# A fused two-block transformer kernel: the places of SBUF tiles modulo 1024 bytes, set by the tiles' role in a matmul

## The chip, the core and the metric

One core of one Trainium2 chip runs the whole kernel. The metric is the device time of one execution in microseconds. [...] SBUF has 128 partitions, and a tile's place is its start address in bytes within a partition; every tile here starts at the same address in all partitions.

## The reference

Two blocks run one after the other on a sequence of 256 tokens with 1024 features, all in float32. Cut to what matters here:

```python
# first block
hn = rms_norm(h, g);  proj = hn @ w_in                  # w_in: 1024 x 8192
merged = sum of three gated branches (spatial gating, convolution, pooling)
h = h + rms_norm(merged @ w_out, g)
f = (silu(hn @ w_gate) * (hn @ w_up)) @ w_ffn_out       # 1024 x 5632, 2816 x 1024
h = h + rms_norm(f, g);  h = h + sigmoid(h @ w_ple_gate) * (p @ w_ple)
# second block, two layers
x = layer_norm(alpha * x + mixer(x))                    # retention, then latent attention
q = x @ w_q;  s = q . sub_keys;  top 16 of 256 candidates per head (8 heads)
h = gelu(u[eidx] . x);  y = sum(gate * h * v[eidx])     # 16384 experts, u and v: 16384 x 1024
x = layer_norm(alpha * x + y)
```

The expert layer (twice) is computed densely: all 16384 rows of `u` meet all tokens, the gates are zero for the experts that a token did not choose, and all 16384 rows of `v` are summed.

## The kernel before

**Weights.** All weights come through one stream (`units`, a list in the order of use). Each unit is a 128x1024 float32 tile: SyncE loads it into one of four `raw` buffers (L139), ScalarE copies it, rounded, into one of three `whi` buffers (L149), and VectorE writes the rest, `raw - whi`, into one of three `wlo` buffers (L164). The activations are split in the same way into a high and a low part. A float32 product is then three TensorE matmuls in the type fp32r: high x high, high x low, low x high.

**Two kinds of matmul.** In every matmul one operand is stationary (128 columns, loaded into the array by a weight load, a PEld record) and one is moving (streamed past it, a MATMUL record). Each matmul has its own weight load, also where the operand is the same as before, and the load for the next matmul runs while this one streams.

- `mm3` (L221 to L223), used by `lin_fm` and by the `u` half of the expert layers: the stationary operand is 128 columns of `whi` or `wlo`, the moving one is 256 tokens of an activation tile (`hl`, `hl3b`, `hlp`, `cqhl`, `phl`). Below: 256-wide. 10,608 matmuls.
- `tm_half` (L285 to L287), used by `lin_tm` and by the `v` half of the expert layers: the stationary operand is 128 tokens of an activation tile (`hl`, `fhl`, `yhl`, `cqhl`, `ohl`, and in the expert layers `ch` and `cl`), the moving one is 512 columns of `whi` or `wlo`. Below: 512-wide. 3072 of them read `ch` and `cl`, 264 `fhl`, 192 `yhl`, 528 `hl`, 96 `ohl`, 42 `cqhl`.

In an expert layer the stretch that reads `u` (256-wide, 128 tiles of weights, 24 matmuls each) comes first, the stretch that reads `v` (512-wide, 128 tiles, 12 matmuls each) second. In the first of them score matmuls (`X` and `q`, float32) and short runs of eight float16 matmuls (`o` with `ohh` and `ohl`, 128 wide) stand between the runs of 24.

**What sets the places.** Tiles are taken from pools. A pool gives out addresses in the order in which its tiles are first asked for, each rounded up to 32 bytes, and the pools `const`, `keep`, `wst` (the weight buffers), `sm` and then those of the stages lie one behind the other. So the place of a tile follows from the sizes of all the tiles ahead of it. `const` starts at byte 16,512. The tile `hl` of the pool `keep` is at byte 21,472 (992 modulo 1024), the weight buffers start at byte 38,944, and since each has 4096 bytes, all ten are at 32 modulo 1024. A slice of 128 columns starts 512 bytes after the one before, a row of 256 tokens 1024 bytes.

The order of the work is written out by hand (weights two units ahead, background work in generators), and nothing in it depends on an address.

Of the kernel before, what the change touches and what calls it, by code (L numbers as in the profile page):

```python
# [10 lines left out]
F32 = mybir.dt.float32  # L11
F32R = mybir.dt.float32r
F16 = mybir.dt.float16
I32 = mybir.dt.int32
# [5 lines left out]
P = 128  # L20
# [72 lines left out]
def fused_kernel(ctx: ExitStack, tc: tile.TileContext, a: dict, out: bass.AP):  # L93
# [3 lines left out]
    const = ctx.enter_context(tc.tile_pool(name="const", bufs=1))  # L97
    keep = ctx.enter_context(tc.tile_pool(name="keep", bufs=1))
    wst = ctx.enter_context(tc.tile_pool(name="wst", bufs=1))
    sm = ctx.enter_context(tc.tile_pool(name="sm", bufs=2))  # L100
# [11 lines left out]

    idle = const.tile([P, 384], F16, name="idle")
    nc.vector.memset(idle, 1.0)

    def C(name, n=None):
        o = COFF[name]
        return cst[:, o:o + (n or dict(CSTS)[name])]
# [217 lines left out]
            nc.vector.scalar_tensor_tensor(out=y, in0=t, scalar=1.5, in1=y, op0=ALU.add, op1=ALU.mult)  # L336
        return y

    eps_t = const.tile([P, 2], F32, name="eps_t")
    nc.vector.memset(eps_t[:, 0:1], EPS1)  # L340
    nc.vector.memset(eps_t[:, 1:2], EPS2)

    def table_ready(func=AF.Sqrt):

        nc.scalar.activation(out=small("rt", 1), in_=eps_t[:, 0:1], func=func)
# [34 lines left out]
    def coeffs_of(mv, eps, root=False, ahead=False):  # L380

        x, nm = small("rx", 2), small("nm", 2)
        if root:
            r = rstd_root(mv[:, :, 1], 1.0, eps, ahead)
        else:
            nc.vector.tensor_scalar(out=x, in0=mv[:, :, 1], scalar1=eps, scalar2=None, op0=ALU.add)
            r = rstd_of(x, 2)
        nc.vector.scalar_tensor_tensor(out=nm, in0=mv[:, :, 0], scalar=-1.0, in1=r, op0=ALU.mult, op1=ALU.mult)
        return r, nm
# [18 lines left out]
    def ax():  # L408
        return ps_ax.tile([P, 512], F32, tag="ax", name="ax")
# [58 lines left out]
    def sincos(ang, sn, cs, pool, n, c1=0.9, c2=1.2):  # L468

        k = pool.tile([P, n], F32, tag="sck", name="sck")  # L470
        nc.vector.tensor_scalar(out=k, in0=ang, scalar1=1.0 / TWO_PI, scalar2=None, op0=ALU.mult)
        nc.vector.tensor_scalar(out=k, in0=k, scalar1=MAGIC, scalar2=None, op0=ALU.add)
        nc.vector.tensor_scalar(out=k, in0=k, scalar1=-MAGIC, scalar2=None, op0=ALU.add)
        yield c1
        for c in (C1, C2, C3):
            nc.vector.scalar_tensor_tensor(out=ang, in0=k, scalar=-c, in1=ang, op0=ALU.mult, op1=ALU.add)
        yield c2
        nc.vector.tensor_scalar(out=ang, in0=ang, scalar1=float(np.float32(3.1415925)), scalar2=float(np.float32(-3.1415925)), op0=ALU.min, op1=ALU.max)
        yield None
        nc.scalar.activation(out=k, in_=ang, func=AF.Abs)  # L480
        nc.scalar.activation(out=sn, in_=ang, func=AF.Sin)
        yield None
        nc.vector.tensor_scalar(out=k, in0=k, scalar1=-1.0, scalar2=math.pi / 2, op0=ALU.mult, op1=ALU.add)
        yield None
        nc.scalar.activation(out=cs, in_=k, func=AF.Sin)
        yield None
# [104 lines left out]
    acct = mx.tile([P, 2, 2, 512], F32, tag="cacct", name="acct")  # L591

    def conv_stats():
        bs = sm.tile([P, 2, 2, 6], F32, tag="cbs", name="cbs", bufs=1)
        for g in range(2):
            while ready["a"] < 4 * g + 4:
                yield None
            yield None
            yield None
            for b in range(2):  # L600
                ps = ax()
                for k in range(4):
                    nc.tensor.transpose(ps[:, k * P:(k + 1) * P], acc[:, 4 * g + k, b * P:(b + 1) * P], ident)
                yield None
                nc.vector.bn_stats(out=bs[:, b, g, :], in_=ps)
                nc.scalar.activation(out=acct[:, g, b, :], in_=ps, func=AF.Copy)
                yield 0.6
        mv = sm.tile([P, 2, 2], F32, tag="mv", name="mv")
        for b in range(2):
            nc.vector.bn_aggr(out=mv[:, b, :], in_=bs[:, b])  # L610
        r, nm = coeffs_of(mv, EPS1, root=True)
        yield 1.6
        for g in range(2):
            nc.scalar.activation(out=acct[:, g, 0, :], in_=acct[:, g, 0, :], func=AF.Identity, scale=r[:, 0:1], bias=nm[:, 0:1])
            nc.vector.tensor_scalar(out=acct[:, g, 1, :], in0=acct[:, g, 1, :], scalar1=r[:, 1:2], scalar2=nm[:, 1:2], op0=ALU.mult, op1=ALU.add)
            yield 0.6
        table_ready(AF.Silu)

    bg += [conv_stats(), conv_taps()]
    lin_fm("w_conv", hl, KD, 16, ev_conv, head=2, produce=[pr_x, pr_x2], budget=BUD["w_conv"], x32=hn32)  # L620

# [108 lines left out]
    for gi in range(4):  # L730
        for f in range(2):
            c = 2 * gi + f
            gp = bank(c % 4)[:, :T]
            for k in range(2):
# [3 lines left out]
                s = slice((t % 8) * P, (t % 8 + 1) * P)  # L738
# [104 lines left out]
    ff, fhl = ff_box["p"], ff_box["fhl"]  # L843
# [38 lines left out]
    decay = tb.tile([P, 4, 2 * T], F32, tag="decay", name="decay")  # L882
    bg.append(tables())
    pT = ff.tile([P, 2, T], F32, name="pT")
    phl = ff.tile([P, 2, 2, T], F32R, name="phl")
    nc.gpsimd.dma_start(out=pT, in_=a["pT"])

# [18 lines left out]
    def ev_ple(i):  # L906
        nc.scalar.activation(out=pple[:, 2 * i:2 * i + 2, :].rearrange("p a t -> p (a t)"), in_=pps[i], func=AF.Copy)

    for f in range(8):
        for k in range(2):  # L910
# [6 lines left out]
            s = slice((t % 8) * P, (t % 8 + 1) * P)  # L917
            mm3(pps[f // 2][:, (f % 2) * T:(f % 2 + 1) * T], (w[0][:, s], w[1][:, s]), (phl[:, 0, k, :], phl[:, 1, k, :]), k == 0, k == 1)
    ev_ple(2)
    ev_ple(3)  # L920
    hlp = ff.tile([P, 2, KD, T], F32R, name="hlp")

    def pr_h2(k):
# [467 lines left out]
        return hl2_box["lt"].after  # L1391


    sc2 = keep.tile([P, 2, 2, 1, 32], F32, name="sc2")
    sn2, cs2 = sc2[:, 0], sc2[:, 1]

    def angles():
        posc = keep.tile([P, 2], I32, name="posc")
        nc.gpsimd.dma_start(out=posc, in_=a["posc"])
        posf = keep.tile([P, 2], F32, name="posf")  # L1400
        ang = keep.tile([P, 64], F32, name="angm")
        for _ in range(16):
            yield None
        nc.vector.tensor_copy(out=posf, in_=posc)
        for b in range(2):
            nc.vector.tensor_scalar(out=ang[:, b * 32:(b + 1) * 32], in0=C("invf64"), scalar1=posf[:, b:b + 1], scalar2=None, op0=ALU.mult)
        yield 2.5
        yield from sincos(ang, sn2.rearrange("p b o f -> p (b o f)"), cs2.rearrange("p b o f -> p (b o f)"), keep, 64, 2.5, 2.5)

    PE0, X = peer(0, hl, lt, hm, [RT, TB], after0, beside_v=[angles()])  # L1410
    lt, hl, hm = hl2_box["lt"], hl2_box["hl"], hl2_box["hm"]

# [14 lines left out]
    ml = ML.enter_context(tc.tile_pool(name="ml", bufs=1))  # L1427
# [5 lines left out]
    for b in range(2):  # L1433
        nc.scalar.activation(out=kvr[:, b, 0:128], in_=psb[b][0][:, 384:512], func=AF.Copy)
        nc.scalar.activation(out=kvr[:, b, 128:320], in_=psb[b][1][:, 0:192], func=AF.Copy)
    cqhl = ml.tile([P, 2, 5, T], F32R, name="cqhl")

    def cq_t(k):
# [8 lines left out]
        cq_t(k)  # L1447

    mjunk = ml.tile([P, 512], F32, name="mjunk")
    rqs = ml.tile([P, 2], F32, name="rqs")  # L1450
    SCL = 192.0 ** -0.5
    ss, x4 = small("ss4", 4), small("x4", 4)

# [281 lines left out]
```

## Time and profile before

| | |
|---|---|
| three timed runs | 2524.02 us median (2523.16 to 2529.32) |
| the profiled execution | 2526.07 us, its span 2524.3 us |
| TensorE, matmuls | 2482.1 us busy (98%), 16,903 records |
| TensorE, weight loads | 2236.3 us (89%), 16,903 records |
| VectorE | 1815.6 us (72%) |
| ScalarE | 1276.8 us (51%) |
| DMA | 441.14 MB, mean 175 GB/s |
[...]

How to read it: a matmul's record reaches from its start to the end of its output, and the next one starts long before that end, so the durations of matmuls overlap and their sum is more than the span. What a matmul costs the engine is the step from its start to the start of the next one. It is taken below from the first and the last start of many like matmuls. Where the steps of two runs of the same shape differ, the durations differ by about as much.

### The profile page before, as it was taken

The page shows a single profiled execution, that of the slowest core. Times are in us where ns is not written, and L with a number is a line of the kernel's source. Part 1 is how long each engine was busy: PE and PEld are TensorE (multiplying, and loading weights), DVE is VectorE, ACT ScalarE, POOL GpSimd, SP SyncE. Part 2 cuts the span into 40 slices and gives each one's busy share as a digit, 9 for nine tenths or more (in the row PEclk, how much of TensorE's full clock was granted, in tenths as well). Part 3 has the DMA queues.
Part 4 walks back from the last instruction along what each step waited for, and adds up shares of the span by engine and source line. Part 5 has one row for each costly group of instructions (what it writes and reads, how often), then busy time and mean ns, then how long its engine had stood idle before and what let it go on. Part 6 is the DMA issues. An engine that isn't in the chain of part 4 may idle for free.

```text
span 2524.3 us, 43428 instructions
## 1 busy us (share of the span) xinstructions
PE 2482.1 (98%) x16903; PEld 2236.3 (89%) x16903; DVE 1815.6 (72%) x3714; ACT 1276.8 (51%) x2161; POOL 9.2 (0%) x21
## 2 busy tenths in 40 slices
PE   8999999999999999999999999999999999999998
PEld 8899899898889999999878888779999999888886
DVE  7988677676656978899555555666978998555555
ACT  5544555563544555544454444544565554444444
POOL 0000000000000000000000000000000000000000
PEclk9999999999999999999999999999999999999999
DMA  6645556555454554545655555525654445655553
GB/s 205 219 147 169 176 164 195 188 192 175 133 177 167 178 190 162 163 163 164 203 184 186 190 187 167 166 77 180 193 191 159 161 160 169 221 187 190 186 190 117
DMA packets 120927, 441.14 MB, mean 175 GB/s; under 512 B 13936, under 2 KB 14320, under 8 KB 119312
## 3 DMA queue, kind: packets, MB, share of 16 engines
q1 hardware_dynamic: 118832, 425.91, 51.8%
q0 software_dynamic: 1888, 12.45, 1.4%
q8 instruction: 132, 2.16, 0.3%
q14 instruction: 75, 0.61, 0.1%
HBM read 433.07 MB, written 5.24 MB: 174 GB/s over the span
## 4 chain that ended last, share of the span: by engine, by line
PE 82%; issue 13%; DMA 2%; ACT 2%; DVE 1%; SPq 0%; POOL 0%; POOLq 0%; ACTq 0%; DVEq 0%
PE bank L287 11%; PE bank L285 11%; PE bank L286 11%; PE bank L221 10%; PE bank L222 10%; PE bank L223 10%; PE lps L221 4%; PE lps L222 4%; PE lps L223 4%; PE lps L270 2%; PE ax L1273 1%; PE ax L1274 1%; DMA X<-in_keys_dram 1%; PE ax L1112 1%; ACT whi L149 1%
## 5 line engine op out<-in xcount | busy, mean ns | idle before, releaser
L164 DVE TENSOR_TENSOR wlo<-raw,whi 128x1024 fp32r<-128x1024 f32 (+1 forms) x797 | 968.1, 1216 | 529.3 <-ACT whi L149 526.7
L149 ACT ACTIVATE whi<-raw 128x1024 fp32r<-128x1024 f32 (+1 forms) x797 | 838.7, 1053 | 723.0 <-PE bank L287 477.4
L221 PE MATMUL bank<-hl,whi 128*128 128x256 f32 x2080 | 597.7, 287 | 4.0 <-ACT hl L550 3.0
L222 PE MATMUL bank<-hl,whi 128*128 128x256 f32 x2080 | 584.7, 281 | 0.3
L223 PE MATMUL bank<-hl,wlo 128*128 128x256 f32 x2080 | 584.4, 281 | 0.3 <-DVE wlo L164 0.3
L285 PE MATMUL bank<-whi,ch 128*128 128x512 f32 x1024 | 404.9, 395 | 1.9 <-ACT ch L323 1.9
L287 PE MATMUL bank<-whi,cl 128*128 128x512 f32 x1024 | 404.8, 395 | 0.1
L286 PE MATMUL bank<-wlo,ch 128*128 128x512 f32 x1024 | 404.5, 395 | 0.0
L221 PEld LDWEIGHTS bank<-hl,whi 128*128 128x128 f32 x2080 | 394.4, 190 | 4.8 <-ACT hl L550 3.3
L222 PEld LDWEIGHTS bank<-hl,whi 128*128 128x128 f32 x2080 | 395.4, 190 | 1.4 <-DVE hl L465 0.5
L223 PEld LDWEIGHTS bank<-hl,wlo 128*128 128x128 f32 x2080 | 392.7, 189 | 1.0 <-DVE wlo L164 0.9
L221 PE MATMUL lps<-hl,whi 128*128 128x256 f32 x1208 | 343.0, 284 | 0.6 <-ACT fhl L834 0.5
L223 PE MATMUL lps<-hl,wlo 128*128 128x256 f32 x1208 | 337.1, 279 | 0.5 <-DVE wlo L164 0.5
L222 PE MATMUL lps<-hl,whi 128*128 128x256 f32 x1208 | 336.9, 279 | 0.0
L285 PEld LDWEIGHTS bank<-whi,ch 128*128 128x128 f32 x1024 | 191.9, 187 | 49.1 <-ACT ch L323 2.8
L287 PEld LDWEIGHTS bank<-whi,cl 128*128 128x128 f32 x1024 | 191.9, 187 | 48.7 <-DVE cl L324 1.8
L286 PEld LDWEIGHTS bank<-wlo,ch 128*128 128x128 f32 x1024 | 191.9, 187 | 46.7
L221 PEld LDWEIGHTS lps<-hl,whi 128*128 128x128 f32 x1208 | 228.9, 189 | 1.5 <-ACT fhl L834 0.7
L222 PEld LDWEIGHTS lps<-hl,whi 128*128 128x128 f32 x1208 | 229.5, 190 | 0.3
L223 PEld LDWEIGHTS lps<-hl,wlo 128*128 128x128 f32 x1208 | 228.7, 189 | 0.8 <-DVE wlo L164 0.7
L1302 ACT ACTIVATE gel<-bank 128x84 f32<-128x84 f32 (+47 forms) x154 | 44.0, 286 | 178.6 <-PE bank L223 178.6
L1304 ACT ACTIVATE X<-bank 128x256 f32<-128x256 f32 (+33 forms) x246 | 76.5, 311 | 105.8 <-PE bank L223 105.8
(420 smaller groups left out, 3063.9 us busy)
## 6 DMA issues: line engine op xcount, KB each, us to landing
raw<-in_p_u_dram SPq DMA_DIRECT2D x256, 512.0 KB, 3.3
raw<-in_p_v_dram SPq DMA_DIRECT2D x256, 512.0 KB, 3.4
raw<-in_w_fi_dram SPq DMA_DIRECT2D x44, 512.0 KB, 4.2
raw<-in_p_q_dram SPq DMA_DIRECT2D x32, 512.0 KB, 3.4
raw<-in_w_gate_dram SPq DMA_DIRECT2D x24, 512.0 KB, 3.3
raw<-in_w_fo_dram SPq DMA_DIRECT2D x22, 512.0 KB, 3.7
raw<-in_w_conv_dram SPq DMA_DIRECT2D x16, 512.0 KB, 4.2
raw<-in_r_qk_dram SPq DMA_DIRECT2D x16, 512.0 KB, 4.2
```

Source lines behind the costliest of these rows:

```text
L149: nc.scalar.activation(out=hi[:, :c], in_=raws[j][:, :c], func=AF.Copy)
L164: nc.vector.tensor_tensor(out=lo[:, :c], in0=r[:, :c], in1=hi[:, :c].bitcast(F32), op=ALU.subtract)
L221: nc.tensor.matmul(ps, w[0], x[0], start=start, stop=False, skip_group_check=True)
L222: nc.tensor.matmul(ps, w[0], x[1], start=False, stop=False, skip_group_check=True)
L223: nc.tensor.matmul(ps, w[1], x[0], start=False, stop=stop, skip_group_check=True)
L270: nc.tensor.matmul(ps[:, :T], w[0][:, s], x32[:, k0 + k, :], start=(k == 0), stop=(k == nk - 1), skip_group_check=True)
L285: nc.tensor.matmul(ps[:, :n], xh, w[0][:, o:o + n], start=first, stop=False, skip_group_check=True)
L286: nc.tensor.matmul(ps[:, :n], xh, w[1][:, o:o + n], start=False, stop=False, skip_group_check=True)
L287: nc.tensor.matmul(ps[:, :n], xl, w[0][:, o:o + n], start=False, stop=last, skip_group_check=True)
L1112: nc.tensor.matmul(p2[:, b * P:(b + 1) * P], q[:, b * P:(b + 1) * P], box["keys"][:, f, :], start=True, stop=True, skip_group_check=True)
L1302: nc.scalar.activation(out=gl_[:, 0:td], in_=ps[:, 0:td], func=AF.Gelu)
L1304: nc.scalar.activation(out=X[:, e, td:], in_=ps[:, td:T], func=AF.Gelu)
```

## The change

No instruction is added, removed or moved: on every engine the two programs as built hold the same instructions with the same shapes and the same waits in the same order. One VectorE copy, of the 128x2 positions, writes into two spare columns of `eps_t` and no longer into a tile `posf`. Only addresses differ. Three unused tiles (`gap1`, `gap2`, `gap3`) and some larger tiles (`cbs`, `sc2`, `rqs`, `eps_t`) shift what comes behind them, and `posc` moves into `const`.

| tile | role | before, modulo 1024 | after |
|---|---|---|---|
| `raw`, `whi`, `wlo` | both | 32 | 64 |
| `hl` of `keep`, `hl3b` | moving, stationary | 992 | 0 |
| `hl` of the first block's branches | moving, stationary | 960 | 0 |
| `hlp` | moving | 128 | 0 |
| `cqhl` | moving, stationary | 512 | 0 |
| `phl` | moving | 0 | 0 |
| `ch`, `cl` | stationary | 0 | 64 |
| `fhl`, `yhl` | stationary | 0 | 64 |
| `ohl` | stationary | 544 | 64 |
| `X`, `q`, `o`, `ohh` and the expert layers' other tiles | float32, float16 | 0 | 64 |

Since slices of weights and of stationary activations start 512 bytes apart, their places repeat modulo 512: `ohl` at 544 has slices at 32 and at 544, as the weights have.

```diff
@@ -112,6 +112,8 @@
     idle = const.tile([P, 384], F16, name="idle")
     nc.vector.memset(idle, 1.0)
+    eps_t = const.tile([P, 4], F32, name="eps_t")
+    posc = const.tile([P, 2], I32, name="posc")
...
-    eps_t = const.tile([P, 2], F32, name="eps_t")
     nc.vector.memset(eps_t[:, 0:1], EPS1)
     nc.vector.memset(eps_t[:, 1:2], EPS2)
...
     def conv_stats():
-        bs = sm.tile([P, 2, 2, 6], F32, tag="cbs", name="cbs", bufs=1)
+        bs = sm.tile([P, 32], F32, tag="cbs", name="cbs", bufs=1)[:, 0:24].rearrange("p (b g s) -> p b g s", b=2, g=2)
...
     pT = ff.tile([P, 2, T], F32, name="pT")
+    ff.tile([P, 240], F32, name="gap1")
     phl = ff.tile([P, 2, 2, T], F32R, name="phl")
...
     ev_ple(3)
+    ff.tile([P, 224], F32, name="gap2")
     hlp = ff.tile([P, 2, KD, T], F32R, name="hlp")
...
-    sc2 = keep.tile([P, 2, 2, 1, 32], F32, name="sc2")
+    sc2 = keep.tile([P, 144], F32, name="sc2")[:, 0:128].rearrange("p (a b o f) -> p a b o f", a=2, b=2, o=1)
...
     def angles():
-        posc = keep.tile([P, 2], I32, name="posc")
         nc.gpsimd.dma_start(out=posc, in_=a["posc"])
-        posf = keep.tile([P, 2], F32, name="posf")
+        posf = eps_t[:, 2:4]
...
+    ml.tile([P, 112], F32, name="gap3")
     cqhl = ml.tile([P, 2, 5, T], F32R, name="cqhl")
...
-    rqs = ml.tile([P, 2], F32, name="rqs")
+    rqs = ml.tile([P, 16], F32, name="rqs")[:, 0:2]
```

## Rows read from the trace of the kernel before

**Rows 1.** The page: busy time, granted clock, the chain by engine.
```profile
PE 2482.1 (98%) x16903; PEld 2236.3 (89%) x16903; DVE 1815.6 (72%) x3714; ACT 1276.8 (51%) x2161; POOL 9.2 (0%) x21
...
PEclk9999999999999999999999999999999999999999
...
PE 82%; issue 13%; DMA 2%; ACT 2%; DVE 1%; SPq 0%; POOL 0%; POOLq 0%; ACTq 0%; DVEq 0%
```

**Rows 2.** Stretches: busy us (instructions) by engine, clock, DMA share, GB/s.
```profile
core 0: us, PE busy (x) PEld busy (x) DVE busy (x) ACT busy (x) POOL busy (x), PEclk, DMA share, GB/s
817.00:1215.00 398.00, 397.22 (x3609) 394.00 (x3609) 347.90 (x860) 209.22 (x416) 0.76 (x2) 1.00 0.52 170
2151.00:2510.00 359.00, 359.00 (x1556) 289.14 (x1556) 196.97 (x253) 173.35 (x255) 0.53 (x1) 1.00 0.57 186
```

**Rows 3.** One line's matmuls, the v half: durations min/median/max ns, first, last start.
```profile
L286 PE MATMUL bank<-wlo,ch x399: 388/396/397, 1259.9 to 1539.8; 128*128 128x512 f32 x200
L286 PE MATMUL bank<-wlo,ch x401: 393/396/397, 2199.8 to 2479.8; 128*128 128x512 f32 x134
```

**Rows 4.** The same view: 512-wide with ohl, all of them, and the last stretch.
```profile
L286 PE MATMUL bank<-wlo,ohl x32: 387/389/397, 1648.4 to 1690.6; 128*128 128x512 f32 x32
L286 PE MATMUL bank<-wlo,ohl x5: 389/389/389, 1687.9 to 1690.6; 128*128 128x512 f32 x5
```

**Rows 5.** Timeline of that last stretch with ohl: start, duration us, instruction.
```profile
1687.90 0.39 PE L286 MATMUL bank<-wlo,ohl 128*128 128x512 f32 x1
...
1690.62 0.39 PE L286 MATMUL bank<-wlo,ohl 128*128 128x512 f32 x1
```

**Rows 6.** One line's matmuls: 512-wide with fhl, yhl and hl (five stretches).
```profile
L286 PE MATMUL bank<-wlo,fhl x84: 393/395/397, 450.3 to 508.4; 128*128 128x512 f32 x84
L286 PE MATMUL bank<-wlo,yhl x55: 392/394/397, 704.0 to 741.8; 128*128 128x512 f32 x55
L286 PE MATMUL bank<-wlo,hl x32: 392/392/397, 291.9 to 313.6; 128*128 128x512 f32 x32
L286 PE MATMUL bank<-wlo,hl x32: 392/392/392, 61.5 to 82.8; 128*128 128x512 f32 x32
L286 PE MATMUL bank<-wlo,hl x32: 397/397/398, 591.0 to 612.6; 128*128 128x512 f32 x32
```

**Rows 7.** One line's matmuls: 256-wide with hl of keep, undisturbed stretches.
```profile
L221 PE MATMUL lps<-hl,whi x111: 276/276/276, 23.5 to 60.9; 128*128 128x256 f32 x111
L221 PE MATMUL lps<-hl,whi x313: 276/276/276, 339.8 to 445.9; 128*128 128x256 f32 x157
L221 PE MATMUL bank<-hl,whi x165: 281/281/281, 831.8 to 889.8; 128*128 128x256 f32 x165
```

**Rows 8.** The same: 256-wide between X and q, and between o.
```profile
L221 PE MATMUL lps<-hl,whi x110: 276/276/561, 766.8 to 816.3; 128*128 128x256 f32 x110
L222 PE MATMUL bank<-hl,whi x600: 277/281/281, 958.6 to 1201.7; 128*128 128x256 f32 x150
L222 PE MATMUL bank<-hl,whi x608: 277/281/281, 1891.0 to 2137.5; 128*128 128x256 f32 x152
```

**Rows 9.** The same: 256-wide with hl of the branches, hlp, cqhl.
```profile
L221 PE MATMUL lps<-hl,whi x33: 277/282/365, 244.8 to 256.7; 128*128 128x256 f32 x33
L221 PE MATMUL lps<-hlp,whi x46: 278/280/385, 528.2 to 544.7; 128*128 128x256 f32 x46
L221 PE MATMUL lps<-cqhl,whi x16: 277/280/387, 1615.5 to 1621.8; 128*128 128x256 f32 x16
```

## The prediction

> **What bounds the kernel now.** I read the page first: TensorE is busy in 98% of the span, 82% of the chain that ended last is its matmuls, and the granted clock is full in every slice [rows 1]. So the matmuls' own pace sets the time, not a wait, and not the lower of the two clock levels. The stretches confirm it for the two largest stages: in the u half of an expert layer TensorE is busy 397.2 of 398 us, in the v half 359.0 of 359, with VectorE at 347.9 and 197.0, ScalarE below that, the DMA share at 0.52 and 0.57 [rows 2]. Whatever changes the step from one matmul to the next in these stages therefore moves the end by as much; the splitting engines and the DMA have room.
>
> Then I read the step itself, from the first and the last start of one line's matmuls; each line is one in three.
>
> - v half, 512-wide, stationary `ch` and `cl` at 0, moving weights at 32: 400 x 3 steps in 280.0 us, 233.3 ns; in the first layer 398 x 3 in 279.9 us, 234.4 ns [rows 3].
> - 512-wide with `ohl`, the one tile whose slices lie at the same place as the weights' (32 and 32 modulo 512): at first up to 397 ns long, then 389 without exception [rows 4]; 12 steps from 1687.90 to 1690.62, 2.72 us, 226.7 ns [rows 5]. A duration of 396 goes with a step of 233.3 and 389 with 226.7: seven ns of either.
> - 512-wide with `fhl` and `yhl`, at 0 like `ch`: 83 x 3 steps in 58.1 us and 54 x 3 in 37.8 us, 233.3 each [rows 6].
> - 512-wide with `hl`, at 480 modulo 512: 392 ns in one stretch and 397 in another, the same tiles at the same places [rows 6].
> - 256-wide with `hl` at 992 and weights at 32, that is 64 higher: 312 x 3 steps in 106.1 us, 113.4 ns, in one stretch, 164 x 3 in 58.0 us, 117.9 ns, in another, with durations of 276 and 281 that don't vary within either [rows 7].
> - 256-wide at the other places (`hl` of the branches, 96 lower than the weights; `hlp`, 96 higher; `cqhl`, 32 lower modulo 512): medians of 280 to 282, never 276 [rows 9].
>
> So a shape has a few fixed paces. The place of the two operands against each other decides which of them occur: 389 only at equal places, 276 only at 64. Where two occur, the pace is kept through a whole stretch, so the way in which a stretch begins picks it. After the float32 score matmuls (`X`, `q`) the 256-wide ones run at a median of 276, after the float16 ones (`o`) at 281, in both layers [rows 8].
>
> **The change part by part.** No instruction moves, no wait is added. Only the differences of places count, and I take it that a shift of both operands by the same 32 bytes does nothing; no row shows this, since all weights lie at 32 now.
>
> 1. *v half.* `ch`, `cl` and the weights come to 64 and 64, the relation of `ohl`. 3072 x (233.3 - 226.7 = 6.6 ns) = 20.4 us, all on the path [rows 2, 3, 5]. Bounds: nothing, if they keep 396; the low end of settling is what `ohl` showed in its first twelve, 396 falling to 389 [rows 4], paid once or twice per layer, below 0.1 us. The cover is there: in that stretch VectorE is busy 197 of 359 us and the DMA share is 0.57 [rows 2], so a pace 3% faster doesn't meet either. Taken: 20.4.
> 2. *`fhl` and `yhl`.* The same step in 264 and 192 matmuls: 456 x 6.6 ns = 3.0 us. Bounds 0 and 3.0; taken 3.0.
> 3. *`hl` of the branches, stationary* (96 matmuls). From 93 steps in 21.7 us, 233.3, to the relation of `hl` in `keep`, which runs at 93 steps in 21.3 us, 229.0, or at about its present pace [rows 6]: 0 to 0.4, taken 0.2.
> 4. *256-wide off place.* 384 with `hl` of the branches, 192 with `hlp`, 120 with `cqhl` and 48 with `phl` come to the relation of 64, so from 280 to 282 to either 276 or 281 [rows 7, 9]. 384 x 1 to 6 ns, 360 x -1 to 4 ns: between 0 and 3.7 us, taken in the middle, 1.9.
> 5. *256-wide with `hl` of `keep`* (9672 with the 192 of `hl3b` aside). The difference stays 64, so both paces stay possible. But `X`, `q`, `o` move by 64 while the weights move by 32: the neighbours at which a stretch begins stand differently, and the choice can fall anew. The after-`o` stretches, 1208 x 3 = 3624 matmuls at 281 [rows 8], could gain 4.5 ns each, 16.3 us; the stretches now at 276 could lose as much each. About 939 + 333 of those lie in the two long stretches [rows 7], which the float16 runs don't enter, and 330 behind `X` and `q` in the first layer [rows 8]. Bounds: -16.3 (and some 4 us more from the undisturbed stretches at 281) and +8. Nearest to the case is what stands there now, the pace after `o`, which did not vary in 1208 rows of one line; so taken: 0.
>
> Sum: 20.4 + 3.0 + 0.2 + 1.9 = 25.5 us. Of the profiled execution's 2526.1 us that leaves 2500.6; the median of the three runs is 2.0 below the profiled one, so **2498 us** is the forecast. `cqhl` as a stationary operand (42 matmuls) and the float32 products keep too few steps to be seen.
>
> **The rivals.**
>
> *The u half turns fast too.* As above, but the float16 matmuls, now at the same place as the weights, leave the stretch behind them at 276, as `X` and `q` do already. For it: both paces occur with one and the same relation [rows 7], and only the way in has to change. Against it: nothing shows the new relation between float16 tiles and weights. 25.5 + 16.3 + about 4 in the stretches that stand at 281 without `o` = 46: 2478 us.
>
> *Half of the gain.* The v half has two paces at equal places, as `hl` has [rows 6], and keeps the upper for part of the time. `ohl` showed 396 before 389 [rows 4]. Half of terms 1 and 2: 2498 + 12 = 2510 us.
>
> *The place does nothing.* The paces would come from something else that differs between the stretches, such as the engines writing beside them, and 397 beside 392 for the same tiles speaks for that [rows 6]. Against it: in three stages with tiles at 0 the median is 394 to 396 [rows 3, 6] and only equal places show 389 as the median. 2524 us. [...]
>
> *Slower: the upper pace everywhere.* The stretches that run at 276 now begin beside tiles that have moved, and fall to 281; the 512-wide ones at equal places keep the 397 that `ohl` and `hl` show at times [rows 4, 6]. Price: (939 + 333 + 330 + about 250 in the second layer) x 4.5 ns = 8.3 us, and 3528 x about 1.5 ns = 5.3 us. 2524 + 14 = 2538 us. It decides only if the v half gains less than those 8 us, that is if the median of its matmuls stays above about 393 ns; with term 1 in full, the loss in the 256-wide ones leaves the kernel faster by some 17 us.
>
> **How the numbers follow.** The forecast, 2498: 0.42. The u half fast too, 2478: 0.26. Half of it, 2510: 0.13. No effect, 2524: 0.11. Slower, 2538: 0.08. The range must hold the first three: their ends are 2478 less the 3 to 8 us that fast paces in the short stretches would add, and 2510 plus half of what the 256-wide ones can lose, so 2470 to 2516, with 0.81 inside. The likeliest alone: 2492 to 2506. Within 0.3% of the time before, about what a measurement of this kernel can tell from no change, are 2516.4 to 2531.6. So faster 0.81, the same 0.11, slower 0.08.
>
> **What would show it right or wrong.** In the profile after, the v half's matmuls (L286 in the rows above, at a line number a little higher) should have a median of 389 and a step of 226.7, and the stretch should end some 10 us earlier per layer. The `fhl` and `yhl` rows should read 389 too. The `hl` of the branches should show 276 or 281, no longer 282. In the u half, 281 after `o` means the forecast, 276 the first rival. Wrong is the argument if the v half stays at 396 (then the place isn't it, or the shift of 32 bytes counts by itself), or if the undisturbed stretch at 340 to 446 us reads other than 276 or 281. Should any row fall below 389 or 276, places count against a boundary and not only against each other.

## The result, and the profile after

The changed kernel takes 2485.84 us (median of four runs, 2484.09 to 2487.74) where the kernel before, measured beside it, takes 2524.69. The ratio is 0.9843, with a 95% interval of 0.9826 to 0.9860. The profiled executions read 2526.07 us before and 2485.69 after, their spans 2524.3 and 2483.9: 40.4 us less, at a mean granted clock of 0.993 and 0.994 of full.

First the page of the kernel after, in the lines of [rows 1]: busy us of each engine, the granted clock in tenths, and the chain that ended last.

```profile
PE 2439.4 (98%) x16903; PEld 2219.1 (89%) x16903; DVE 1812.3 (73%) x3714; ACT 1277.2 (51%) x2161; POOL 9.2 (0%) x21
...
PEclk9999999999999999999999999999999999999999
...
PE 90%; issue 5%; DVE 2%; ACT 2%; DMA 2%; SPq 0%; POOL 0%; POOLq 0%; DVEq 0%; ACTq 0%
```

The same 16,903 matmuls now fill 42.7 us less, with TensorE at the same 98% and the clock at 9 tenths or more in every slice. VectorE and ScalarE are within 3.3 us of what they were. So no engine was relieved; the matmuls follow each other more closely. In the chain, matmuls now make up 90% for 82, and the share in which no wait can be seen is 5% for 13.

Next the two halves of the expert layers, in the windows of the changed kernel in which they run (u, v, u, v).

```profile
core 0: us, PE busy (x) PEld busy (x) DVE busy (x) ACT busy (x) POOL busy (x), PEclk, DMA share, GB/s
810.00:1205.00 395.00, 394.22 (x3635) 390.34 (x3634) 349.56 (x866) 211.58 (x419) 1.06 (x2) 1.00 0.54 176
1205.00:1560.00 355.00, 353.78 (x1584) 290.97 (x1583) 204.50 (x283) 178.88 (x265) 0.00 (x0) 1.00 0.57 186
1740.00:2130.00 390.00, 389.22 (x3574) 384.64 (x3573) 346.40 (x843) 210.41 (x415) 0.53 (x1) 1.00 0.55 178
2130.00:2470.00 340.00, 340.00 (x1518) 282.12 (x1517) 192.20 (x247) 168.70 (x248) 0.53 (x1) 1.00 0.57 189
```

Against [rows 2], TensorE is as full as it was and the granted clock is 1.00, with more matmuls to the microsecond: 3635 in 395 us for 3609 in 398, and 1518 in 340 for 1556 in 359. VectorE stands at 349.6 of 395 us in the u half, so it still has room.

Then the matmuls themselves, by the line that answers to L286 before (now L288; each line is one in three). The columns are the durations in ns (least, median, most) and the first and last start in us.

```profile
L288 PE MATMUL bank<-wlo,ch x352: 388/389/397, 1259.9 to 1499.9; 128*128 128x512 f32 x176
L288 PE MATMUL bank<-wlo,ch x368: 389/389/389, 2190.0 to 2439.5; 128*128 128x512 f32 x184
L288 PE MATMUL bank<-wlo,fhl x88: 389/389/395, 446.8 to 506.0; 128*128 128x512 f32 x88
L288 PE MATMUL bank<-wlo,yhl x56: 389/389/395, 699.5 to 736.9; 128*128 128x512 f32 x56
```

In the second layer 367 x 3 steps take 249.5 us, 226.6 ns each, where [rows 3] gave 233.3. `fhl` and `yhl` come from 395 and 394 [rows 6] to 389, too.

One caution on such rows. Away from equal places the durations run through several values in turn (393, 394, 396 and 397 ns with `ch` before), and one line's median need not stand for the others. In [rows 6] a median of 392 goes with 229.0 ns a step at 61 us (93 steps in 21.3 us) and with 233.3 at 292 us (93 in 21.7). Where the two disagree, the step decides.

Last, the 256-wide ones (now L223 and L224): the undisturbed stretch of [rows 7] at 340 us, the stretch that stood at 281 without `o`, and the stretches between `o` in both layers [rows 8].

```profile
L223 PE MATMUL lps<-hl,whi x307: 276/276/357, 334.9 to 439.8; 128*128 128x256 f32 x154
L223 PE MATMUL bank<-hl,whi x180: 281/281/364, 820.2 to 883.7; 128*128 128x256 f32 x180
L224 PE MATMUL bank<-hl,whi x600: 276/276/281, 950.9 to 1186.7; 128*128 128x256 f32 x150
L224 PE MATMUL bank<-hl,whi x592: 276/276/281, 1875.1 to 2107.6; 128*128 128x256 f32 x198
```

The last two were 281 throughout in the kernel before and are now 276. The same 600 rows of the first layer, with the `o` runs between them, take 235.8 us; they took 243.1.

**Where the 40 us went.** Both traces hold the same matmuls in the same order, so the time from each start to the next can be compared one by one and summed by kind:

| matmuls | before, us | after, us | difference | the prediction's term |
|---|---|---|---|---|
| v half, 512-wide, `ch` and `cl`, both layers | 718.3 | 698.4 | -19.9 | 1: -20.4 |
| 512-wide, `fhl` and `yhl` | 106.6 | 103.6 | -3.0 | 2: -3.0 |
| 512-wide, `hl` and `cqhl` | 134.7 | 135.1 | +0.4 | 3: -0.2 |
| 256-wide, `hlp`, `cqhl`, `phl`, and `hl` in the first block's stages before 320 us | 205.7 | 202.3 | -3.4 | 4: -1.9 |
| 256-wide, `hl` in the u halves | 735.5 | 719.4 | -16.1 | 5: 0 |
| 256-wide, `hl` elsewhere | 318.5 | 319.9 | +1.4 | 5: 0 |
| everything else, waits with it | | | +0.2 | |

The fourth row also holds 936 matmuls with `hl` of `keep`, which term 4 doesn't count; they moved by some 0.2 us or less.

### The profile page after: what moved, and what is told of

Read it like the earlier page. It is cut to its first block, busy times and chain, and to the rows that moved or that the text cites. A ratio compares the mean times of both kernels' runs of the same rounds, so it can differ in the third digit from the quotient of the medians.

```text
span 2483.9 us, 43428 instructions
## 1 busy us (share of the span) xinstructions
PE 2439.4 (98%) x16903; PEld 2219.1 (89%) x16903; DVE 1812.3 (73%) x3714; ACT 1277.2 (51%) x2161; POOL 9.2 (0%) x21
## 4 chain that ended last, share of the span: by engine, by line
PE 90%; issue 5%; DVE 2%; ACT 2%; DMA 2%; SPq 0%; POOL 0%; POOLq 0%; DVEq 0%; ACTq 0%
PE bank L289 12%; PE bank L287 12%; PE bank L288 12%; PE bank L223 10%; PE bank L224 10%; PE bank L225 10%; PE lps L223 6%; PE lps L225 6%; PE lps L224 6%; PE lps L272 2%; PE ax L1276 1%; PE ax L1277 1%; DMA X<-in_keys_dram 1%; ACT whi L151 1%; PE ax L1115 1%
## 5 line engine op out<-in xcount | busy, mean ns | idle before, releaser
L223 PE MATMUL bank<-hl,whi 128*128 128x256 f32 x2080 | 592.1, 285 | 4.0 <-ACT hl L551 3.2
L224 PE MATMUL bank<-hl,whi 128*128 128x256 f32 x2080 | 579.2, 278 | 0.3
L225 PE MATMUL bank<-hl,wlo 128*128 128x256 f32 x2080 | 578.3, 278 | 0.5 <-DVE wlo L166 0.5
L287 PE MATMUL bank<-whi,ch 128*128 128x512 f32 x1024 | 398.9, 390 | 2.0 <-ACT ch L325 2.0
L289 PE MATMUL bank<-whi,cl 128*128 128x512 f32 x1024 | 398.7, 389 | 0.3 <-DVE cl L326 0.2
L288 PE MATMUL bank<-wlo,ch 128*128 128x512 f32 x1024 | 398.4, 389 | 0.0
L223 PEld LDWEIGHTS bank<-hl,whi 128*128 128x128 f32 x2080 | 391.8, 188 | 4.9 <-ACT hl L551 3.5
L224 PEld LDWEIGHTS bank<-hl,whi 128*128 128x128 f32 x2080 | 392.1, 189 | 1.4 <-DVE hl L466 0.5
L223 PE MATMUL lps<-hl,whi 128*128 128x256 f32 x1208 | 342.9, 284 | 1.0 <-ACT fhl L835 0.6
L224 PE MATMUL lps<-hl,whi 128*128 128x256 f32 x1208 | 337.0, 279 | 0.0
L223 PEld LDWEIGHTS lps<-hl,whi 128*128 128x128 f32 x1208 | 228.6, 189 | 1.8 <-ACT fhl L835 0.7
L225 PEld LDWEIGHTS lps<-hl,wlo 128*128 128x128 f32 x1208 | 229.0, 190 | 0.7 <-DVE wlo L166 0.7
L224 PEld LDWEIGHTS lps<-hl,whi 128*128 128x128 f32 x1208 | 229.0, 190 | 0.3
L288 PEld LDWEIGHTS bank<-wlo,ch 128*128 128x128 f32 x1024 | 192.2, 188 | 39.7
```

What stands on the lines that cost most here:

```text
L223: nc.tensor.matmul(ps, w[0], x[0], start=start, stop=False, skip_group_check=True)
L224: nc.tensor.matmul(ps, w[0], x[1], start=False, stop=False, skip_group_check=True)
L225: nc.tensor.matmul(ps, w[1], x[0], start=False, stop=stop, skip_group_check=True)
L287: nc.tensor.matmul(ps[:, :n], xh, w[0][:, o:o + n], start=first, stop=False, skip_group_check=True)
L288: nc.tensor.matmul(ps[:, :n], xh, w[1][:, o:o + n], start=False, stop=False, skip_group_check=True)
L289: nc.tensor.matmul(ps[:, :n], xl, w[0][:, o:o + n], start=False, stop=last, skip_group_check=True)
```

## The experiments

Two things had to be told apart. One is what counts for the time: the places against each other, the places themselves, or the role. The other is what turned the pace behind `o`, which the prediction had left as it was. Except where a diff says so, each kernel is the changed kernel with one more edit, and "the difference" is the place of one tile minus that of another, modulo 256 bytes unless said.

### One tile alone

The kernel before, with one buffer of the pool `sm` made 32 bytes longer. All that lies behind `sm`'s `cbs` moves up by 32 bytes; `hl` and the weights stay at 992 and 32.

```diff
-        bs = sm.tile([P, 2, 2, 6], F32, tag="cbs", name="cbs", bufs=1)
+        bs = sm.tile([P, 32], F32, tag="cbs", name="cbs", bufs=1)[:, 0:24].rearrange("p (b g s) -> p b g s", b=2, g=2)
```

> The kernel before with the tile cbs alone taken from 96 to 128 bytes. All tiles of the stages come 32 bytes higher: ch, cl, fhl, yhl, X, q, o to 32, the branches' hl to 992. The weights stay at 32, hl of keep at 992. So every difference of places that matters is that of the changed kernel, but each place lies 32 bytes lower. If only the difference counts: v half at a step of 226.7 ns (durations 389), fhl and yhl 389, the u half behind o at 276 ns, and about 2487 us (2484 to 2491; hlp, cqhl, ohl and phl are at new differences, a few us of doubt). If the places 0 and 64 count by themselves (a boundary every 64 bytes): v half nearer to the 396 ns of before, the u half at 281, 2510 to 2525 us.

Measured: 2483.95 us (four runs, 2480.92 to 2485.51), ratio 0.9836 (0.9814 to 0.9858). The rows of this kernel for the v half, the u half behind `o` and `hlp` (its line numbers are those of the kernel before):

```profile
L286 PE MATMUL bank<-wlo,ch x368: 389/389/389, 2189.8 to 2439.4; 128*128 128x512 f32 x184
L222 PE MATMUL bank<-hl,whi x601: 276/276/281, 950.9 to 1187.5; 128*128 128x256 f32 x151
L222 PE MATMUL bank<-hl,whi x592: 276/276/281, 1874.9 to 2107.5; 128*128 128x256 f32 x198
L222 PE MATMUL lps<-hlp,whi x48: 278/281/287, 526.7 to 544.3; 128*128 128x256 f32 x48
```

Here `hl`, the weights and the tiles of the expert layers lie 32 bytes lower than in the changed kernel, with the same differences, and the v half and the u half behind `o` run as there, at 389 and 276. So a common shift of 32 bytes does nothing that these rows show, and the differences are what counts. Of the changed kernel's edits, the 32 bytes between the weights and the stages' tiles carry all of the gain that can be measured. `hlp`, which this edit puts at a difference of 128, stays at 281; in the changed kernel, with a difference of 64, its median is 276.

### The expert layers' tiles moved against the weights: 96, 128 and 256 bytes

A pad ahead of `q`, `o`, `ohh`, `ohl`, `ch` and `cl` in their pool; the weights, `hl` and `X` stay.

```diff
             box["pp"] = PE.enter_context(tc.tile_pool(name=f"pp{layer}", bufs=1))
+            box["pp"].tile([P, 24], F32, name="gap4")   # 96 bytes; 32 for 128, 64 for 256
```

> The changed kernel with 96 unused bytes ahead of the expert layers' small tiles: ch, cl, q, o, ohh, ohl at 160, that is 96 above the weights at 64. X and everything else stay. If the difference counts modulo 128, 96 is what they had before (0 against 32 is -32): v half back to durations of 394 to 396 and a step of 233.3 ns (+20 us), the u half behind o back to 281 (+16 us), in all about 2522 us. If it counts modulo 512 or 1024, 96 is a new difference and nothing says that the old paces return; equally if a neighbour other than these tiles sets the pace, 2486 us.

> The changed kernel with 128 unused bytes there: ch, cl, q, o, ohh, ohl at 192, that is 128 above the weights. If the pattern repeats every 128 bytes, this is the same as 0: v half 389 ns, step 226.7, u half behind o at 276, 2486 us. If equal places modulo 512 or 1024 are needed: v half at 392 to 397, 2500 to 2510 us.

> The changed kernel with ch, cl, q, o, ohh, ohl 256 bytes above the weights' place (128 gave a step of 232.4 ns in the v half, so the pattern does not repeat every 128). If it repeats every 256: v half back at 226.7 ns (389), 2486 us. If it repeats every 512 or 1024 only: 229 to 235 ns in the v half, 2495 to 2520 us. The u half behind o: unknown in either case, 276, 281, or the pace that stood ahead of the o run, as at 128.

Measured, one run each: 2527.70, 2511.67 and 2486.22 us. The rows are those of the v half and of the u half behind `o` in the first and the second layer, for the pad of 96 bytes first; the last one stands ahead of the first `o` in the second layer.

```profile
L288 PE MATMUL bank<-wlo,ch x385: 392/397/400, 2210.0 to 2479.9; 128*128 128x512 f32 x193
L224 PE MATMUL bank<-hl,whi x576: 280/281/281, 965.6 to 1198.9; 128*128 128x256 f32 x192
L224 PE MATMUL bank<-hl,whi x598: 280/281/281, 1895.0 to 2137.6; 128*128 128x256 f32 x200
L224 PE MATMUL bank<-hl,whi x36: 281/281/281, 1877.0 to 1889.3; 128*128 128x256 f32 x36
```

The pad of 128 bytes, with the runs ahead of the first `o` (they end at 949 and 1885 us) and behind it apart:

```profile
L224 PE MATMUL bank<-hl,whi x29: 281/281/281, 944.9 to 955.9; 128*128 128x256 f32 x29
L224 PE MATMUL bank<-hl,whi x580: 281/281/281, 961.8 to 1197.1; 128*128 128x256 f32 x194
L224 PE MATMUL bank<-hl,whi x32: 276/276/279, 1875.8 to 1886.9; 128*128 128x256 f32 x32
L224 PE MATMUL bank<-hl,whi x592: 276/276/279, 1892.4 to 2124.9; 128*128 128x256 f32 x198
L288 PE MATMUL bank<-wlo,ch x360: 390/393/404, 2209.7 to 2459.9; 128*128 128x512 f32 x180
```

The pad of 256 bytes:

```profile
L288 PE MATMUL bank<-wlo,ch x368: 389/389/389, 2189.8 to 2439.4; 128*128 128x512 f32 x184
L224 PE MATMUL bank<-hl,whi x599: 276/276/281, 950.9 to 1186.3; 128*128 128x256 f32 x200
```

Two readings follow.

*The v half.* At a difference of 96 its step is 384 x 3 in 269.9 us, 234.3 ns; at 128 it is 359 x 3 in 250.2, 232.3; at 256 it is 226.7 again. The first of these looked like a pattern that repeats every 128 bytes, since -32 and 96 are slow alike; the pad of 128 shows that it doesn't. 0 and 256 run alike, so 256 bytes is the period that fits these runs, and in them nothing calls for the 1024 of the table of places.

*The u half.* No edit here touches its own two operands; only what stands between its runs of 24 has moved. Yet at 96 all of it is back at 281, at 256 all of it is at 276, and at 128 the first layer is at 281 and the second at 276. In that last kernel the `o` runs hand on the pace that they met: 281 ahead of them and behind them in one layer, 276 ahead and behind in the other. The kernels before and after show the two other cases. These rows are from the second layer, ahead of the first `o` and behind it, in the kernel before (L222) and in the changed one (L224):

```profile
L222 PE MATMUL bank<-hl,whi x36: 276/276/276, 1877.9 to 1889.8; 128*128 128x256 f32 x36
L222 PE MATMUL bank<-hl,whi x29: 278/281/281, 1892.8 to 1904.7; 128*128 128x256 f32 x29
```

```profile
L224 PE MATMUL bank<-hl,whi x34: 281/281/281, 1855.0 to 1866.7; 128*128 128x256 f32 x34
L224 PE MATMUL bank<-hl,whi x32: 276/276/281, 1871.8 to 1884.0; 128*128 128x256 f32 x32
```

Before, with the `o` tiles 32 bytes below the weights, the `o` run turned a fast stretch slow; after, at the same place as the weights, it turns a slow one fast. Each layer has 64 such runs, and in the traces the rule holds for all 128: at -32 the matmuls settle slow behind every one of them, at 0 and at 256 fast, at 128 at the pace ahead. At 96 all of them are slow, but so is the pace ahead of the first one in both layers; whether `o` at 96 sets the slow pace or hands it on isn't shown.

### `hl` against the weights: 0, 128, 192 and 256 bytes

A longer or shorter `sc2` behind `hl` moves the weights and all stages' tiles together; `hl` of `keep` stays at 0. The difference, 64 in the changed kernel, becomes 0, 128, 192 or 256.

```diff
-    sc2 = keep.tile([P, 144], F32, name="sc2")[:, 0:128].rearrange("p (a b o f) -> p a b o f", a=2, b=2, o=1)
+    sc2 = keep.tile([P, 128], F32, name="sc2")[:, 0:128].rearrange("p (a b o f) -> p a b o f", a=2, b=2, o=1)   # 160, 176, 192
```

> The changed kernel with sc2 64 bytes smaller: weights and all stage tiles come to 0 where they were at 64, so that hl of keep (at 0) stands at the same place as the weights and not 64 lower; v half, fhl, yhl and o stay at equal places with the weights. It asks for the pace of 256-wide matmuls at equal places, which no row has shown. If equal places are best for any pair of operands: 276 ns everywhere, also in the stretches that now hold 281 (a third of the u half and more), 2470 to 2480 us. If 256-wide matmuls need the 64: 280 to 286 throughout, 2500 to 2530 us, with the v half unchanged at 226.7 either way.

> The changed kernel with sc2 64 bytes larger: weights and all stage tiles 64 bytes higher, so hl of keep stands 128 below the weights and all other differences stay. It asks whether 64 is the only difference at which 256-wide matmuls reach 276 ns (0 gave 283 and a step of 120). If 64 alone does: steps of 117 to 121 ns, about 2505 to 2530 us. If any difference of 64 or more does: 113.3 to 117.8, 2470 to 2490 us.

> The same with sc2 128 bytes larger: hl of keep 192 below the weights. If 64 alone is good: steps of 117 to 121 ns, 2505 to 2530 us. If the pattern repeats every 128, as it does not for the v half: 113.3 or 117.8 as in the changed kernel, about 2486 us.

> The same with sc2 192 bytes larger: hl of keep 256 below the weights. If the pattern repeats every 256, this is equal places, a step of 120 ns throughout the 256-wide stretches with hl and about 2530 us. If it repeats every 512 only: another pace, between 113 and 121 ns, 2470 to 2530 us.

Measured: at 0, 2529.50 us (ten runs, 2526.79 to 2534.47), ratio 1.0022 (1.0012 to 1.0031); at 128, 192 and 256 one run each, 2524.13, 2515.71 and 2526.71. The rows are from 360 to 430 us, inside a stretch of 256-wide matmuls, and from 60 to 86 us, where `hl` is the stationary operand of 512-wide ones: first the changed kernel, then the differences 0, 128, 192 and 256.

```profile
L224 PE MATMUL lps<-hl,whi x206: 276/276/276, 360.0 to 429.7; 128*128 128x256 f32 x103
L288 PE MATMUL bank<-wlo,hl x32: 392/392/392, 60.7 to 82.0; 128*128 128x512 f32 x32
```

```profile
L224 PE MATMUL lps<-hl,whi x195: 283/283/283, 360.0 to 429.9; 128*128 128x256 f32 x195
L288 PE MATMUL bank<-wlo,hl x32: 389/389/398, 63.6 to 84.7; 128*128 128x512 f32 x32
L288 PE MATMUL bank<-wlo,ch x368: 389/389/389, 2209.9 to 2459.4; 128*128 128x512 f32 x184
```

```profile
L224 PE MATMUL lps<-hl,whi x198: 279/281/285, 359.7 to 429.9; 128*128 128x256 f32 x198
```

```profile
L224 PE MATMUL lps<-hl,whi x199: 279/279/279, 359.9 to 429.9; 128*128 128x256 f32 x199
L288 PE MATMUL bank<-wlo,hl x32: 393/396/398, 64.2 to 85.9; 128*128 128x512 f32 x32
```

```profile
L224 PE MATMUL lps<-hl,whi x195: 283/283/283, 359.8 to 429.7; 128*128 128x256 f32 x195
```

In steps, the 256-wide ones go at 113.3 ns (205 x 3 in 69.7 us) at a difference of 64, at 120.1 (194 x 3 in 69.9) at 0, at 118.8 at 128 and at 117.8 at 192; 256 reads 283 like 0. So a 64-byte difference is the only one of these with the fast pace, and an equal place is the worst for this shape. It is the best for the other: at 0 the 512-wide ones with `hl` come from 229.0 ns a step to 226.9 (93 in 21.1 us). The v half doesn't move (389 in its row, and also at 128, 192 and 256, where `ch` and the weights shift together), so its 20 us stay, and what is lost lies in the 256-wide ones: each of the two u halves is 15.0 us longer than in the changed kernel, and the other stretches with `hl` lose the rest. That undoes the whole gain.

### `X` moved against `q` and the weights

In the kernel before, each run of 24 behind a `q`, `X` pair was fast; in the changed one they alternate. The rows: one such run of the kernel before (L222), then two neighbouring runs of the changed kernel (L224).

```profile
L222 PE MATMUL lps<-hl,whi x8: 276/276/283, 791.7 to 794.1; 128*128 128x256 f32 x8
```

```profile
L224 PE MATMUL lps<-hl,whi x8: 276/276/282, 784.5 to 786.9; 128*128 128x256 f32 x8
L224 PE MATMUL lps<-hl,whi x8: 281/281/281, 787.7 to 790.2; 128*128 128x256 f32 x8
```

Both `q` and `X` had stood 32 bytes below the weights and now stand at their place. The edit puts `X` 32 bytes below again and leaves `q`, `o` and the rest where the change put them; the changed kernel itself ran beside it.

```diff
+            pb.tile([P, 56], F32, name="gapx")
             X = box["X"] = pb.tile([P, P, T], F32, name="X")
             box["pp"] = PE.enter_context(tc.tile_pool(name=f"pp{layer}", bufs=1))
+            box["pp"].tile([P, 8], F32, name="gap4")
```

> As the changed kernel, but the tile X of both layers (and with it the keys that the q stage multiplies) moves 32 bytes lower against q and the weights, modulo 256; q, o and every other stage tile keep their places. Theory A (the place of a float32 run's operands against the weights decides the pace of the 256-wide products behind it): the runs of 24 behind a q,X pair, which alternate between 118 and 114 ns a step in the changed kernel, go at 114 each time, as in the kernel before, where X stood 32 bytes below the weights; the q stages get 1 to 1.5 us shorter each, the 552 steps behind the last pair get about 2.5 us shorter if they start fast and stay so, and the time falls by 3 to 8 us, to 2478 to 2483. Theory B (only the places of the two operands of a product itself count, and the choice between the paces is a matter of when the re-entry comes): the same alternation, 2484 to 2488. Theory C (q and X want the same place for the pair itself): the float32 pairs get longer, 2487 to 2492.

> The changed kernel unaltered, beside the run with X 32 bytes lower on the same chip, so that the two are compared with each other. Every theory: 2484 to 2488 us, 0.984 to 0.985 of the kernel before, the 512-wide steps 226.7 ns, the 256-wide runs behind an o run 113.3 ns.

Measured: 2485.73 us with `X` lower (five runs, 2478.21 to 2492.26) and 2489.93 without (five, 2483.59 to 2491.86); ratios to the kernel before of 0.9836 (0.9814 to 0.9857) and 0.9844 (0.9826 to 0.9862). The two don't differ by more than their spread. With `X` lower the runs of 24 still alternate:

```profile
L224 PE MATMUL lps<-hl,whi x8: 276/276/282, 784.0 to 786.4; 128*128 128x256 f32 x8
L224 PE MATMUL lps<-hl,whi x8: 281/281/281, 787.2 to 789.7; 128*128 128x256 f32 x8
```

So theory A falls for `X`: the place of the moving operand of the pair is not what decides here. What stays is `q`, the stationary one, which took the same step from -32 to 0. The kernels with pads had moved just that: in their `q` stages, which come ahead of the first `o`, `q` alone stands elsewhere against `X`, `hl` and the weights. At 96 all of the runs between 783 and 816 us are slow, at 128 they alternate (the last two rows), and at 256, too:

```profile
L224 PE MATMUL lps<-hl,whi x80: 281/281/281, 783.5 to 815.4; 128*128 128x256 f32 x80
```

```profile
L224 PE MATMUL lps<-hl,whi x7: 281/281/281, 783.8 to 785.9; 128*128 128x256 f32 x7
L224 PE MATMUL lps<-hl,whi x8: 276/276/279, 787.0 to 789.4; 128*128 128x256 f32 x8
```

So the place of `q` counts for the pace behind the pair.

The changed kernel's second profile (span 2488.2 us) is 4.3 us longer than its first, and 4.2 us of that lie in one stretch of 110 us, from about 335 us on, which the pads and the edit of `X` don't reach. Its middle:

```profile
L224 PE MATMUL lps<-hl,whi x199: 281/281/281, 359.8 to 429.8; 128*128 128x256 f32 x199
```

That is the slow pace, with the places that gave 276 in the first profile. This stretch begins behind waits for other engines (0.6 us for `fhl` of ScalarE in the first profile), and which pace it takes differs from run to run, with some 4 us hanging on it. The kernels with pads of 96 and 128 bytes had it slow as well (4.2 us each against the changed kernel's first profile), so their times are not to be read more finely than that.

## Why the prediction was right, and the step in which it was off

The forecast was 2498 us and the time is 2485.84, inside the range and 12 us below the forecast; the first rival stood at 2478, 8 us on the other side, and what came about is that rival's mechanism. The time lies in the range because the range was drawn to hold the first rival too; it lies outside the 2492 to 2506 that were called the likeliest. Each step in turn:

- **What bounds the kernel** held. TensorE stays full at 98%, the granted clock is 1.00 in the four windows above (the lower of the two levels in the traces, 0.50, was granted in short stretches such as 12 to 15 us), and a nanosecond of step was a nanosecond of time, times the count: the differences of the table add up to the 40.4 us of the spans.
- **Term 1 and term 2** held: 19.9 and 3.0 us for 20.4 and 3.0. The row with the five `ohl` in it [rows 4, 5] was the right one to take the new pace from: 226.7 is what long runs of 512-wide matmuls at equal places come to in every row here that shows them. "Then 389 without exception" was read too simply, though. The `ohl` matmuls are interrupted, at first after every twelve, and behind each interruption up to ten of them take 224 to 236 ns each before they settle; so in the changed kernel, at equal places as before, their row has a median of 392. The v half has long runs, and there it costs nothing that can be seen. Term 3 was nothing to speak of, as said: the 96 with the `hl` of the branches, from 290 us on, still step at 233.4. The row of `ohl` after:

```profile
L288 PE MATMUL bank<-wlo,ohl x32: 387/392/397, 1624.8 to 1667.0; 128*128 128x512 f32 x32
```

- **Term 4** gave 3.4 us for 1.9, near the end of 3.7 that the prediction had written beside it.
- **The assumption ahead of the terms**, that a common shift of 32 bytes does nothing, is shown by the one-tile kernel (389 and 276 as in the changed one, 2483.95 us).
- **Term 5 is the step that failed.** It was taken as 0, from "the pace after `o`, which did not vary in 1208 rows of one line", and it came to -14.7 us: -16.1 in the u halves and +1.4 elsewhere. The bound of -16.3 was worked out rightly from the 3624 matmuls after `o`. What was wrong was the value between the bounds. 1208 rows that all begin in the same way are one observation of that beginning, not 1208; and the change altered just that, the place of the `o` tiles against the weights, from -32 to 0. The kernels with pads show that this place governs the pace: behind `o` it is slow at -32 (281 ns), fast at 0 and 256 (276), handed on at 128.
- **The first rival** had the mechanism but 4 us too much: the stretches that stood at 281 without `o` did not turn fast with the rest. The longest of them, from 832 us on [rows 7], need not take its pace from the pair of `q` and `X` ahead of it. In the kernel before, the matmuls behind that pair were fast, and the slow pace came in at a single late one (a step of 0.27 us at 829.91, with a wait of 0.2 us for `wlo` in it); in the changed kernel the pace is slow ahead of the late one there (a step of 0.17 us at 823.28) and behind it; with the pad of 96 bytes it is slow ahead and fast behind. So in the first and the last of these kernels the pace changed behind the pair, in the first of them at a wait. The rows: before, ahead of that wait and behind it (L222), then behind it with the pad of 96 (L224).

```profile
L222 PE MATMUL bank<-hl,whi x8: 276/276/282, 827.2 to 829.6; 128*128 128x256 f32 x8
L222 PE MATMUL bank<-hl,whi x169: 281/281/281, 830.5 to 889.9; 128*128 128x256 f32 x169
```

```profile
L224 PE MATMUL bank<-hl,whi x156: 276/276/276, 836.0 to 888.7; 128*128 128x256 f32 x156
```

- **Half of the gain** and **the place does nothing** fell with the v half's 389, a median in both layers and without exception in the second layer's row. On the second: with the same instructions in the same order, the step of the v half was 233.3 ns at a difference of -32, 226.7 at 0, 234.3 at 96 and 232.3 at 128.
- **Slower everywhere** was right in that a re-entry can lose the fast pace (the pairs with `q` did: in each layer six runs of 24 went at 117.8 ns a step for 113.5, some 0.6 us) and wrong in the size, since the long undisturbed stretches kept theirs in the first profile. A version that does lose was at hand: `hl` at the weights' own place, 2529.50 us.

**What stays open.** The pace behind an insertion depends on the place of its tiles; this was shown for -32, 0, 128 and 256, and for `q` at 96. The places are given against the weights, but `hl` was 64 below the weights in all of these kernels, so that they might as well be counted against `hl`; no run tells the two apart. For `o` the moving and the stationary tile always moved together. `q` was moved alone, but not to -32. Why an insertion at the weights' place sets the fast pace when it is `o` and flips it when it is `q` and `X`, and what in a wait chooses, is not settled by any run. Neither is the cause of the slower steps themselves: the runs show that the difference of the places counts, and not by what mechanism.

## What to carry to other kernels

Where TensorE is full (98% here) and the granted clock is 1.00, read the step from start to start by shape and by tile; if one shape shows two steps, compare the start addresses of its two operands, modulo 256 as it fitted here, before looking for waits. Here a 3% cheaper step (226.7 ns for 233.3) came with 32 bytes in one tile, equal places for the 512-wide matmuls and a difference of 64 for the 256-wide ones. And when a row is used to say that a pace won't change, ask how many different beginnings it has seen, not how many instructions.

## What the runs showed of the hardware

- At a granted clock of 1.00 the step of the fp32r matmuls of these kernels went with the difference of their operands' places: 0 and 256 bytes ran alike (226.7 ns and 226.7 for 512-wide, durations of 283 and 283 for 256-wide), 0 and 128 didn't (226.7 and 232.3, 120.1 and 118.8). With a 512-wide moving operand: 226.7 ns at a difference (stationary minus moving) of 0, 229.0 or 233.4 with `hl` at 64 below, 233.3 at -32, 234.3 at 96, 232.3 at 128. With a 256-wide one: 113.3 or 117.8 at 64 (weights minus moving), 117.8 at 192, 118.8 at 128, 120.1 at 0.
- At a difference of 64 two paces of the 256-wide shape, 113.3 and 117.8 ns, both kept going over long runs of like matmuls (206 rows at 276 in one profile and 199 at 281 in another, from 360 to 430 us). Short insertions of another type, 0.43 us long (`o`) or 0.36 (`X` and `q`), switched between them or handed them on, with the places of their own tiles: behind `o` 281 at -32, 276 at 0 and 256, and the pace ahead at 128. The pace also changed at a wait of 0.2 us, from 276 to 281 at 830 us in the kernel before.
- One stretch of 110 us took either pace in two profiles of the same program, a difference of 4.2 us.
